# Second block: 28 feature-major projections as 14 seven-product pairs in a stage of their own, stored to DRAM, with the 32 gates dealt out 6, 10 and 16 over three mixers

## The chip, the cores and the metric

One core of one Trainium2 chip runs the whole program. The metric is device time in microseconds, the median of the runs of one kernel. Work is split over five engines: PE (matmul), with PEld for its weight loads, DVE, ACT, POOL and SP, which here issues the DMA transfers.

## The reference, cut to what matters

Two transformer blocks follow each other on x of 1024 tokens by 1024 features. The first (an mLSTM with window attention, then a convolutional FFN) is not touched. In the second, `xn = rmsnorm(x)` feeds one wide projection, and four mixers and four gates are computed from it:

```python
xn = rmsnorm_2(x, attn_norm_g)
proj = xn @ w_in                       # pool 512, dilated 3x768, stick 3x512, s5 512 columns
y_pool = pool_mixer(u_pool, pool_w, pool_scale)
y_dil  = dilated_attention(qkv_dil, rel_bias)     # 3 groups of 4 heads, dilation 1, 4, 16 (blocks of 128)
y_sb   = stick_breaking_attention(qkv_sb)         # 4 heads of 128
y_s5   = s5_mixer(u_s5, ...)
merged = 0
for bi, yb in enumerate((y_pool, y_dil, y_sb, y_s5)):
    gate = sigmoid(xn @ w_gate[bi])               # 1024 x 1024 each
    merged = merged + gate * (yb @ w_branch[bi])
x = x + merged @ w_out
hn = rmsnorm_2(x, ffn_norm_g); gu = hn @ w_up
x = x + (silu(gu[:, :F]) * gu[:, F:]) @ w_down    # F = 2816
return rmsnorm_2(x, final_norm_g)
```

## The kernel before, in words

**Layout and products.** x lies feature-major: eight tiles of 128 features by 1024 tokens. Every matmul is in float32 made of two rounded halves: a tile `t` is split into `hi` (rounded by ACT, L382) and `lo = t - hi` (DVE, L383), and a product is `hi*hi + hi*lo + lo*hi`, lines L358, L360 and L362 in `gemm`. A projection of 128 output features, from `load_w` (one 512 KB weight load, split in two halves of 512 columns) and `gemm`, is 8 x 3 x 2 = 48 matmuls of 512 columns. A gate, made by `gate` through `fill`, is 48 matmuls as well.

**The seven-product pair.** `pair` (L886) takes two such projections together: the two weight tiles are a 2 x 2 block matrix, the normed x another one (features 0 to 511 and 512 to 1023 by left and right half of the tokens), and the product of the two is made from seven half-size products of 12 matmuls each, 84 in all, where two projections by `gemm` are 96. For that POOL makes sums of weight blocks, and DVE adds the products up. The second FFN's `up` already runs 22 pairs this way.

**Order of the second block.** `block2_norm` (from L1566) normalises x, leaves its halves `xh`, `xl` and sends the residual `xd` to DRAM; it runs two half projections `early` ahead. Then come three mixers: `stick` (stick-breaking attention), `dilated`, and `s5`, in which the pool mixer runs along as a generator `means`. Then merge and FFN.

**Fills.** Where a mixer would leave PE waiting, the code calls `fill` (L300), which takes the next of the 32 gates off a list, computes it and spills it to DRAM. `stick` takes 1, `dilated` 15 and `s5` 16. The 28 feature-major projections (8 of `stick`, 12 + 4 of `dilated`, 4 of the pool mixer) stand between them and serve the same way. The order on each engine is fixed when the program is built: a scheduler, with priorities by place in the program, decides which matmuls of fills and projections stand between those of a mixer, and every engine then runs its list in order.

**The dilated mixer.** For each group g = 0, 1, 2 there is a setup: `oh,tab` matmuls (L1772) gather the relative bias, which is stored to a DRAM buffer (ED) and loaded back as `hk`; `hk` is transposed by PE (L1781); four `dqk` projections and, for g = 1 and 2, two `dvf` projections run, whose `dvf` tiles are transposed into `vd` by `turn`. The loop of eight steps n follows. One step is: scores on PE (L1850, four matmuls in the program, eight records in the trace); bias, maximum and sum on DVE (L1853, four, then L1856); four exps on ACT (L1858); four transposes on PE (L1863); a copy on ACT (L1866); the product with the values on PE (L1875); and copies out (L1878, L1880). In groups 0 and 1 most steps have 256 keys ("wide"), in group 2 all have 128 ("narrow"). A fill stands after every second step. After the loops `mst` is transposed (L1887), two more fills stand in group 2, and the weights of the groups (`E`, POOL, L1932) are spread by `E,selr` matmuls (L1943).

**s5.** Four quarters q: POOL builds `CL` (L2110) and `BL` (to L2134), PE transposes `BL` (L2140), DVE runs a recurrence to `H`, PE contracts it (L2211, L2212), then gelu and transposes. `CL` has one buffer, so the next quarter's POOL work starts when L2212 has read it. Each quarter has four gates or fewer and one step of the pool mixer, with its projection.

## Time and profile before

| what | value |
|---|---|
| median of 3 runs | 3456.14 us (3456.09 to 3456.77) |
| the profiled execution's own time | 3452.84 us |
| its span on the core | 3451.0 us |
| PE busy | 3312.0 us, 96% of the span |
| PEld, DVE, ACT, POOL busy | 76%, 61%, 38%, 19% |
| DMA | 348.60 MB, mean 101 GB/s |

The span is cut into stretches in the rows below: `block2_norm` ends about 1411 us, `stick` about 1659, `dilated` about 2112, `s5` (with its gated output) about 2490; the second FFN's norm is at 2741 to 2793, and its seven-product pairs from 2810 to 3170. A row of the busy times by stretch reads: from:to and length, then busy time of PE, PEld, DVE, ACT and POOL with the count of instructions, then the granted TensorE clock (1.00 is full), the DMA share and GB/s. A row of the timeline reads: start, duration, engine, line, operation, output<-input, shapes, and in brackets how long the engine was idle before it and what released it. In a row of one line's instructions, three durations in ns are the least, the median and the most.

### The profile page before, as it was taken

Reading aid. Unit: us, or ns where it says so; the run is one execution under the profiler, and the core shown is the slowest. Engines: PE = TensorE matmul, PEld = TensorE weight load, DVE = VectorE, ACT = ScalarE, POOL = GpSimd, SP = SyncE. Lnnn points to the kernel's source line nnn. Section 1 sums busy time; section 2 is a strip of 40 time slices with the busy share of each in tenths; the row PEclk is TensorE's granted clock in tenths of the full one; section 3 lists DMA queues with packets and bytes.
Section 4 is the critical chain, followed back from the end, with each engine's and each line's share of the span. In section 5 each row is a group of like instructions: output and inputs, shape, how many; then the busy total and the mean of one; then the engine's idle time right before and its main releaser. Section 6 shows DMA issues by size and latency. Waiting matters only on the chain. (4 is left out here: it accounts for less than half of the span.)

```text
span 3451.0 us, 42496 instructions
## 1 busy us (share of the span) xinstructions
PE 3312.0 (96%) x15699; PEld 2635.8 (76%) x15699; DVE 2092.2 (61%) x3955; ACT 1311.0 (38%) x2471; POOL 654.7 (19%) x510
## 2 busy tenths in 40 slices
PE   6999998989999999899999999999999989999998
PEld 4797776768888777777877778787878768888777
DVE  8746787686565797677332237466265764434886
ACT  5224655454444334356242332222222443333332
POOL 3200000152221441200000002221032142321530
PEclk9999999999999999999999999999999999999999
DMA  6545112422221432201121112222464322223232
GB/s 235 199 151 181 42 59 90 143 85 81 80 80 58 168 94 84 98 31 37 51 65 52 63 55 97 72 90 87 163 227 156 132 98 86 79 85 126 89 93 78
DMA packets 139953, 348.60 MB, mean 101 GB/s; under 512 B 16713, under 2 KB 41697, under 8 KB 139745
## 3 DMA queue, kind: packets, MB, share of 16 engines
q1 hardware_dynamic: 139744, 345.88, 29.7%
q8 instruction: 124, 2.03, 0.2%
q14 instruction: 85, 0.69, 0.1%
HBM read 270.67 MB, written 75.16 MB: 100 GB/s over the span
## 5 line engine op out<-in xcount | busy, mean ns | idle before, releaser
L382 ACT ACTIVATE wh<-w 128x512 fp32r<-128x512 f32 (+1 forms) x508 | 308.4, 610 | 1035.2 <-PE mm L360 734.5
L383 DVE TENSOR_TENSOR wl<-w,wh 128x512 fp32r<-128x512 f32 (+1 forms) x508 | 365.3, 723 | 512.6 <-ACT wh L382 491.5
L358 PE MATMUL mm<-bh,wh 128*128 128x512 f32 x1376 | 532.9, 401 | 26.7 <-ACT a L904 6.2
L362 PE MATMUL mm<-bh,wl 128*128 128x512 f32 x1376 | 523.6, 396 | 4.0 <-DVE wl L383 3.8
L360 PE MATMUL mm<-bl,wh 128*128 128x512 f32 x1376 | 526.3, 396 | 0.2 <-DVE bl L383 0.2
L358 PEld LDWEIGHTS mm<-bh,wh 128*128 128x128 f32 x1376 | 259.8, 189 | 110.2 <-DVE x L2364 11.7
L362 PEld LDWEIGHTS mm<-bh,wl 128*128 128x128 f32 x1376 | 259.7, 189 | 68.7 <-DVE wl L383 7.6
L362 PE MATMUL mm<-xh,wl 128*128 128x512 f32 x944 | 311.7, 401 | 0.0
L358 PE MATMUL mm<-xh,wh 128*128 128x512 f32 x944 | 308.9, 403 | 1.9 <-DVE sql L386 1.9
L360 PEld LDWEIGHTS mm<-bl,wh 128*128 128x128 f32 x1376 | 260.0, 189 | 57.8 <-DVE bl L383 0.6
L360 PE MATMUL mm<-xl,wh 128*128 128x512 f32 x944 | 304.1, 399 | 0.0
L896 POOL TENSOR_TENSOR ws<-w 128x512 f32<-128x512 f32 x44 | 67.0, 1523 | 850.3 <-DMA w<-in_w_up_dram 510.0
L362 PEld LDWEIGHTS mm<-xh,wl 128*128 128x128 f32 x944 | 176.8, 188 | 43.9 <-issue 5.8
L360 PEld LDWEIGHTS mm<-xl,wh 128*128 128x128 f32 x944 | 177.8, 189 | 40.8 <-issue 2.0
L358 PEld LDWEIGHTS mm<-xh,wh 128*128 128x128 f32 x944 | 174.3, 188 | 44.8 <-issue 5.1
L382 ACT ACTIVATE wh<-ws 128x512 fp32r<-128x512 f32 x176 | 110.7, 630 | 202.0 <-PE mm L360 171.9
L362 PE MATMUL ax<-bh,wl 128*128 128x512 f32 x416 | 165.3, 397 | 4.2 <-DVE wl L383 4.2
L360 PE MATMUL ax<-bl,wh 128*128 128x512 f32 x416 | 165.9, 399 | 2.2 <-DVE bl L383 2.1
L358 PE MATMUL ax<-bh,wh 128*128 128x512 f32 x416 | 165.8, 398 | 1.6 <-ACT bh L382 1.6
L383 DVE TENSOR_TENSOR wl<-ws,wh 128x512 fp32r<-128x512 f32 x176 | 137.6, 783 | 27.0 <-ACT wh L382 26.8
L1553 DVE SCALAR_TENSOR_TENSOR x<-mm,adaT,x 128x512 f32<-128x512 f32 (+1 forms) x104 | 85.4, 828 | 40.3 <-PE mm L362 40.0
L1932 POOL TENSOR_TENSOR E<-e,seld 32x1024 fp32r<-32x1024 f32 x3 | 8.2, 2733 | 476.8 <-issue 476.2
(639 smaller groups left out, 6849.9 us busy)
## 6 DMA issues: line engine op xcount, KB each, us to landing
w<-in_w_up_dram SPq DMA_DIRECT2D x88, 512.0 KB
wa<-in_w_ada_dram SPq DMA_DIRECT2D x64, 512.0 KB
w<-in_w_out_dram SPq DMA_DIRECT2D x32, 512.0 KB
w<-in_w_gate_dram SPq DMA_DIRECT2D x32, 512.0 KB
gd<-gf SPq DMA_DIRECT2D x32, 512.0 KB
g<-gd SPq DMA_DIRECT2D x32, 512.0 KB
y<-y SPq DMA_DIRECT2D x28, 512.0 KB
w<-in_w_down_dram SPq DMA_DIRECT2D x24, 512.0 KB
```

The source lines that it names most:

```text
L358: nc.tensor.matmul(ps, lhsT=wh, rhs=xh[k], start=s, stop=False, **kw)
L360: nc.tensor.matmul(ps, lhsT=wh, rhs=xl[k], start=False, stop=False, **kw)
L362: nc.tensor.matmul(ps, lhsT=wl, rhs=xh[k], start=False, stop=e, **kw)
L382: first = nc.scalar.activation(hi, src, AF.Copy)
L383: nc.vector.tensor_tensor(lo, src, hi.bitcast(F32), ALU.subtract)
L896: nc.gpsimd.tensor_tensor(t, x, y, op)
L1553: add = lambda m, x, ps: nc.vector.scalar_tensor_tensor(x, ps, self.adaT[:, 40 + m : 41 + m], x, ALU.mult, ALU.add)
L1932: eng.tensor_tensor(E.rearrange("p (n t) -> p n t", n=8), e.bitcast(F32).unsqueeze(1).to_broadcast([32, 8, P]), seld[:, 256:264].unsqueeze ...
```

## The change

`block2_norm` no longer runs `early` nor makes `xd`; it spills the raw x (`xr`), and prepares the operands of the seven products (`factors2`: B11, B21, T1, B22, T2, T3, T4, as in the second FFN). A new stage `project2` runs the 28 projections as 14 pairs, through `rows` (the loop that was in `up`). Each result is scaled, for the dilated mixer also reordered by dilation (ACT writes it token-residue major, and the store then has runs of 512 bytes for dilation 4, of 256 bytes for 8), and stored to DRAM. Between pairs `residual` loads `xr`, makes `xd` and stores it. The mixers load their inputs from DRAM where the projections stood. The constant GATES, by which gates could run in the new stage too, is empty. FILL says after which steps a fill stands in `dilated`: n = 1, 4 and 6 of each group, and one behind the groups, 10 in all; in `stick` 6 (one per head, and one more in heads 0 and 1); `s5` keeps 16.

```diff
...
+FILL = ((1, 4, 6), (1, 4, 6), (1, 4, 6), (0, 1))
+
+GATES = ()
...
     def block2_norm(self, xs, out):
...
-        def early(m):
-            hi, lo = self.load_w(A["w_sbqk"][m], D)
-            ps = self.pax()
-            self.gemm(hi, lo, [(ps, self.xh2[0], self.xl2[0])])
-            self.first.append((ps, hi, lo))
...
+                nc.sync.dma_start(self.xr[m][:, sl], xs[m][:, sl])
                 if h == 1:
-                    norm(m, 0)
-            if h == 1:
-                early(0)
-                early(4)
...
-        for k in range(KC):
-            self.dump(f"x2{k}", xs[k])
-            nc.vector.scalar_tensor_tensor(xs[k], xs[k], self.smc("final_norm", k), r1, ALU.mult, ALU.mult)
-            nc.sync.dma_start(self.xd[k], xs[k])
...
+    def project2(self, fp, B, steps):
...
+        jobs = [(sq(h), sq(4 + h)) for h in range(4)] + [(po(0), po(1)), (po(2), po(3))] + [(dq(2 * i), dq(2 * i + 1)) for i in range(6)] + [(dv(0), dv(1)), (dv(2), dv(3))]
+        jobs += [(ga(*GATES[i]), ga(*GATES[i + 1])) for i in range(0, len(GATES), 2)]
+
+        def run(j, *first):
+            def store(i, h, src):
+                _, d, scale, s, f = jobs[j][i]
+                if i == 0 and s == 1 and scale == 1.0 and f == AF.Copy:
+                    nc.sync.dma_start(d[:, h * HT : (h + 1) * HT], src)
+                    return
+                t = self.sm.tile([P, HT], F32, tag=("it", "dt")[h], name=self.nm("pj"), bufs=2)
+                nc.scalar.activation(t.rearrange("p (s l) -> p l s", s=s), src.rearrange("p (l s) -> p l s", s=s), f, scale=scale)
+                n = HT // s
+                nc.sync.dma_start(d.rearrange("p (s l) -> p s l", s=s)[:, :, h * n : (h + 1) * n], t.rearrange("p (s l) -> p s l", s=s))
...
+        def residual():
+            if left:
+                k = left.pop(0)
+                x = self.big("x")
+                nc.sync.dma_start(x, self.xr[k])
+                nc.vector.scalar_tensor_tensor(x, x, self.smc("final_norm", k), self.r1, ALU.mult, ALU.mult)
+                nc.sync.dma_start(self.xd[k], x)
...
+        self.rows(run, len(jobs), steps, residual)
...
@@ stick
                 if h < 3:
-                    qk, _ = heads(h + 1)
-                else:
-                    self.fill(None, turn=1, raw=True)
+                    qk, _ = heads(h + 1, fp)
+                self.fill(fp, turn=1, raw=True)
                 for _ in run[1]:
                     pass
+                if h in FILL[3]:
+                    self.fill(fp, turn=1, raw=True)
...
@@ dilated
                     for m in range(2):
-                        hi, lo = self.load_w(A["w_dvf"][2 * (g - 1) + m], D)
-                        ps = self.pmm()
-                        self.gemm(hi, lo, self.xtargets(ps, self.xh2, self.xl2))
                         t = self.big("dvf")
-                        nc.scalar.activation(t.rearrange("p (s l) -> p l s", s=dil), ps.rearrange("p (l s) -> p l s", s=dil), AF.Copy)
+                        nc.sync.dma_start(t, self.dvd[2 * (g - 1) + m])
...
                 for m in range(4):
-                    hi, lo = self.load_w(A["w_dqk"][4 * g + m], D)
...
+                    nc.sync.dma_start(t, self.dqd[4 * g + m])
...
-                if g == 0:
-                    self.fill(fp)
...
-                    if n % 2:
+                    if n in FILL[g]:
                         self.fill(fp)
...
                 if g == 2:
                     with tc.issue_after(last.ins):
-                        self.fill(fp)
                         self.fill(fp)
...
@@ pool mixer, in s5
         for g in range(4):
-            hi, lo = self.load_w(A["w_pool"][g], D)
-            ps = self.pmm()
-            self.gemm(hi, lo, self.xtargets(ps, self.xh2, self.xl2))
             u = self.big("u")
-            nc.scalar.activation(u, ps, AF.Copy)
+            nc.sync.dma_start(u, self.ud[g])
```

How this moves instructions is seen at two places. The first is PE in the loop of dilated group 2. Here is a part of one step of the kernel before: scores (L1850), transposes (L1863), and between them L358, L360 and L362, which are matmuls of a gate (`mm` from `xh`, `xl`).

```order
L1850 MATMUL ax_16619<-dk_16383,dq_16249 128x128
L1850 MATMUL ax_16618<-dk_16456,dq_16310 128x128
L1850 MATMUL ax_16619<-dk_16456,dq_16310 128x128
L362 MATMUL mm_16658<-xh_11165,wl_16651 128x512 x2
L358 MATMUL mm_16658<-xh_11166,wh_16650 128x512 x2
L360 MATMUL mm_16658<-xl_11174,wh_16650 128x512 x2
L362 MATMUL mm_16658<-xh_11166,wl_16651 128x512 x2
L1863 MATMUL ax_16633<-const,ds_16616 128x128
L358 MATMUL mm_16658<-xh_11167,wh_16654 128x512
L1863 MATMUL ax_16633<-const,ds_16616 128x128
```

And the same place in the changed kernel, where L1926 is the scores, L1939 the transposes and L1951 the product with the values; it is the start of group 2's loop, from the last `turn` (L1900) on.

```order
L1900 MATMUL ax_17343<-const,dvf_17317 128x128 x4
L1926 MATMUL ax_17355<-dk_17335,dq_17319 128x128
L1926 MATMUL ax_17356<-dk_17335,dq_17319 128x128
L1926 MATMUL ax_17355<-dk_17349,dq_17321 128x128
L1926 MATMUL ax_17356<-dk_17349,dq_17321 128x128
L1939 MATMUL ax_17370<-const,ds_17353 128x128 x4
L1951 MATMUL ax_17377<-dpt_17375,vd_17313 64x128 x4
L1926 MATMUL ax_17386<-dk_17335,dq_17319 128x128
```

From there to the end of group 2's eight steps no matmul of a gate stands on PE; before, 192 did. The three gates that the program text places in group 2's loop stand on PE ahead of it.

The second place is PE in the setup of group 2, around the transposes of `hk`, in the kernel before (L1781).

```order
L358 MATMUL mm_16139<-xh_11163,wh_16131 128x512 x2
L360 MATMUL mm_16139<-xl_11171,wh_16131 128x512 x2
L1781 MATMUL ax_16044<-hk_16042,const 128x256
L362 MATMUL mm_16139<-xh_11163,wl_16132 128x512
L1781 MATMUL ax_16050<-hk_16048,const 128x256
L362 MATMUL mm_16139<-xh_11163,wl_16132 128x512
L358 MATMUL mm_16139<-xh_11164,wh_16131 128x512 x2
```

In the changed kernel the transposes of `hk` are L1869.

```order
L362 MATMUL mm_17707<-xh_11170,wh_17703 128x512 x2
L364 MATMUL mm_17707<-xl_11178,wh_17703 128x512 x2
L366 MATMUL mm_17707<-xh_11170,wl_17704 128x512 x2
L1869 MATMUL ax_17291<-hk_17289,const 128x256
L1869 MATMUL ax_17297<-hk_17295,const 128x256
L1869 MATMUL ax_17303<-hk_17301,const 128x256
L1869 MATMUL ax_17309<-hk_17307,const 128x256
L1900 MATMUL ax_17323<-const,dvf_17315 128x128 x4
```

Between `oh,tab` and the first scores of group 2 stood 288 matmuls of gates and projections, 236 of them behind the first `hk` transpose; now 28 stand there, all ahead of it, and L1900 follows at once.

Counted in the same way over the whole dilated mixer, matmuls of gates and projections are, before and now: group 0 setup 193 and 37, loop 192 and 130; group 1 setup 288 and 50, loop 192 and 134; group 2 setup 288 and 28, loop 192 and 0; behind the groups up to `E,selr` 96 and 48. That is 1441 and 427.

## Rows read from the trace of the kernel before

**Rows 1.** Busy time by stretch: stick, dilated, s5, and the pairs of the FFN.

```profile
1411.00:1659.00 248.00, 245.49 (x1075) 183.26 (x1073) 168.30 (x356) 122.64 (x251) 4.79 (x8) 1.00 0.13 46
1659.00:2112.00 453.00, 450.87 (x2350) 346.94 (x2350) 136.32 (x378) 143.12 (x341) 8.20 (x3) 0.99 0.20 62
2112.00:2490.00 378.00, 374.42 (x1782) 310.41 (x1782) 211.28 (x633) 100.56 (x174) 65.71 (x81) 1.00 0.30 97
...
2810.00:3170.00 360.00, 359.65 (x1551) 291.12 (x1552) 150.44 (x229) 131.75 (x210) 97.34 (x71) 1.00 0.24 85
```

**Rows 2.** One line's instructions: SP's stores of each pair in the second FFN.

```profile
L1636 SPq EVENT_SEMAPHORE  x18: 17/7273/7276, 2838.4 to 3167.9; - x18
L1636 SPq DMA_DIRECT2D y<-a x18: 319/327/327, 2838.4 to 3169.4; - x18
```

**Rows 3.** One line's instructions: ACT's copies of two neighbouring projections.

```profile
L1807 ACT ACTIVATE dvf<-mm x2: 2020/2022/2023, 1817.0 to 1828.1; 128x1024 f32<-128x1024 f32 x2
```

**Rows 4.** Busy time by stretch: the norms ahead of stick and ahead of the FFN.

```profile
1375.00:1411.00 36.00, 26.62 (x115) 20.20 (x114) 33.67 (x43) 17.62 (x28) 21.43 (x13) 0.91 0.30 102
...
2741.00:2793.00 52.00, 43.28 (x176) 32.81 (x175) 47.36 (x68) 25.25 (x44) 19.61 (x12) 0.94 0.11 36
```

**Rows 5.** Timeline of PE: the `oh,tab` matmuls that open groups 0, 1 and 2.

```profile
1659.14 0.80 PE L1772 MATMUL ax<-oh,tab 32*4 32x384 f32 x2
...
1801.98 0.80 PE L1772 MATMUL ax<-oh,tab 32*4 32x384 f32 x2
...
1942.23 0.48 PE L1772 MATMUL ax<-oh,tab 32*4 32x384 f32 x1
```

**Rows 6.** One line's instructions: the scores of groups 0, 1 and 2.

```profile
L1850 PE MATMUL ax<-dk,dq x64: 272/376/480, 1730.4 to 1791.8; 64*128 64x256 f32 x56, 64*128 64x128 f32 x8
...
L1850 PE MATMUL ax<-dk,dq x64: 272/374/480, 1874.2 to 1931.8; 64*128 64x128 f32 x32, 64*128 64x256 f32 x32
...
L1850 PE MATMUL ax<-dk,dq x64: 272/272/374, 2013.6 to 2066.5; 64*128 64x128 f32 x64
```

**Rows 7.** Timeline of PE, DVE and ACT: one step of group 2.

```profile
2044.95 0.71 PE L1850 MATMUL ax<-dk,dq 64*128 64x128 f32 x8
...
2050.15 0.66 PE L1875 MATMUL ax<-dpt,vd 128*64 128x128 f32 x8
2050.74 0.71 PE L1850 MATMUL ax<-dk,dq 64*128 64x128 f32 x8
...
2045.88 0.28 DVE L1853 CUSTOM_DVE_ANT_0 ds<-ax,bias 128x128 f32<-128x128 f32 x1
...
2047.10 0.40 ACT L1858 ACTIVATE ds<-ds,nm 128x128 f32<-128x128 f32 x1 [0.95 <-DVE nm L1856]
...
2048.56 0.19 ACT L1858 ACTIVATION_READ_ACCUMULATOR ds<-ds,nm 128x1 f32 x1
...
2049.32 0.60 ACT L1866 ACTIVATE dpt<-ax 128x512 f32<-128x512 f32 x1 [0.57 <-PE ax L1863]
```

**Rows 8.** Timeline of PE: scores of two neighbouring wide steps of group 0.

```profile
1747.15 1.14 PE L1850 MATMUL ax<-dk,dq 64*128 64x256 f32 x8
...
1754.59 1.14 PE L1850 MATMUL ax<-dk,dq 64*128 64x256 f32 x8
```

**Rows 9.** One line's instructions: the `hk` transposes of group 2, ahead of its scores.

```profile
L1781 PE MATMUL ax<-hk,const x8: 378/379/454, 1955.1 to 1960.1; 128*128 128x256 f32 x8
```

**Rows 10.** Timeline of PE: the first of the `E,selr` matmuls that end dilated.

```profile
2098.12 0.50 PE L1943 MATMUL ax<-E,selr 32*128 32x512 f32 x1
```

**Rows 11.** Busy time by stretch: ten microseconds of the `E,selr` matmuls.

```profile
2101.00:2111.00 10.00, 9.74 (x22) 6.52 (x22) 10.00 (x14) 2.12 (x2) 0.00 (x0) 0.50 0.49 166
```

**Rows 12.** Timeline of POOL and PE: one quarter of s5.

```profile
2289.48 2.16 POOL L2110 TENSOR_TENSOR CL<-C,Lrs 128x1152 f32<-128x1152 f32 x1 [44.66 <-PE ax L2212]
...
2303.55 2.42 POOL L2134 TENSOR_TENSOR BL<-BL,BT 128x1024 f32<-128x1024 f32 x1
...
2312.80 0.27 PE L2140 MATMUL ax<-const,BL 128*128 128x128 f32 x1
...
2351.00 0.39 PE L2212 MATMUL ax<-CL,rt 128*128 128x128 f32 x2
```

More of the change, by code (lines that the diff above doesn't have):

```diff
@@ L966, in up, with rows @@
         run = lambda j, *first: self.pair(fp, W[j], W[NF + j], B, lambda a: hidden(j, a), gated, *first)
+        self.rows(run, NF, steps)
+        return out
+    def rows(self, run, n, steps, each=lambda: None):
         p, q = self.pmm(), self.pmm()
         g = [run(0, (p[:, 0:HT], q[:, HT:T])), run(1, (p[:, HT:T], None)), run(2, (q[:, 0:HT], None))]
-        for n in range(6):
-            if n > 1:
+        for i in range(6):
+            if i > 1:
                 next(steps)
-            for i in g:
-                next(i)
+            for r in g:
+                next(r)
         next(steps)
-        for i in g:
-            next(i)
+        for r in g:
+            next(r)
         cur = run(3)
@@ L979, in up @@
             next(cur)
-        for j in range(4, NF):
+        for j in range(4, n):
+            each()
             new = run(j)
@@ L988, in up @@
         next(cur)
-        return out
     def down(self, fp, W, xd, yd, add):
@@ new lines, in block2_norm, with factors2, split @@
+            row = self.rstd_twice(self.r1[:, sl], r2[:, sl], acc[:, 0:HT], acc[:, HT:T])
+        return B, self.factors2(xs, B, norm, row)
+    def factors2(self, xs, B, norm, row):
+        nc = self.nc
+        L, R = slice(0, HT), slice(HT, T)
+        sub = lambda eng, o, x, y: eng.tensor_tensor(o, x, y, ALU.subtract)
+        pairs = list(zip(xs[:4], xs[4:]))
+        def split(name, k, t):
+            if name not in B or len(B[name][0]) <= k:
+                pair = [self.half_tiles(2, n) for n in ("bh", "bl")]
+                for i in range(2):
+                    B.setdefault(name, ([], []))[i].extend(pair[i])
+            hi, lo = B[name]
+            self.split(t, hi[k], lo[k])
+        for k, (x, y) in enumerate(pairs):
+            norm(k, R, row)
+            nc.sync.dma_start(self.b12[k], x[:, R])
+            t = self.sm.tile([P, HT], F32, tag="it", name=self.nm("t1"), bufs=2)
+            sub(nc.vector, t, x[:, R], x[:, L])
+            split("T1", k, t)
+        yield
+        for k, (x, y) in enumerate(pairs):
+            norm(k + 4, R)
+            sub(nc.gpsimd, x[:, R], y[:, R], x[:, R])
+            split("B22", k, y[:, R])
+        yield
+        for k, (x, y) in enumerate(pairs):
+            nc.vector.tensor_tensor(x[:, L], x[:, R], x[:, L], ALU.add)
+            split("T2", k, x[:, L])
+        yield
+        for k, (x, y) in enumerate(pairs):
+            sub(nc.gpsimd, y[:, L], y[:, L], x[:, L])
+            split("T3", k, x[:, R])
+        yield
+        for k, (x, y) in enumerate(pairs):
+            split("T4", k, y[:, L])
+        yield
@@ L1833, in dilated @@
                         turn(m - 1)
-                nt = [self.big("num") for _ in range(2)]
-                if g == 0:
-                    self.fill(fp)
+                nt = [fp.tile([P, T], F32, name=self.nm("num")), self.big("num")]
                 for n in range(8):
```

89 lines of the change are left out of this document (50 added, 39 removed).

## The prediction

> **What bounds the kernel now.** I read the busy times by stretch first. In stick PE is busy 245.5 of 248.0 us, in dilated 450.9 of 453.0, in s5 374.4 of 378.0, and in the FFN's pairs 359.7 of 360.0 [rows 1]. So everywhere around the change the time is PE's work, and a matmul taken away seems to be worth its full price. But that table cannot say what PE would wait for if it had less to do. For this I read, second, the timeline of single steps in the mixers, where the matmuls of gates and projections stand inside chains of DVE and ACT work [rows 7, 8, 12], and third the order of PE before and now, which tells how many such matmuls are left in each place. The sum is then: work removed, less the waiting that the removed work had covered.
>
> **Work removed.** The price of a pair comes from the FFN's own pairs: its stores run from 2838.4 to 3169.4 us, 18 of them, so 331.0 / 17 = 19.47 us each [rows 2], which is 0.232 us for each of 84 matmuls. The price of a projection is the distance of two neighbours, 1828.1 − 1817.0 = 11.1 us for 48 matmuls [rows 3]. The new stage costs 14 × 19.47 = 272.6 us, the 28 projections that go cost 28 × 11.1 = 310.8 us: **−38.2 us**. The gates only move. Per matmul I use 0.2315 us.
>
> **The way into the pairs.** Before, PE idled 36.00 − 26.62 = 9.4 us in the stretch of the norm, with two half projections as cover. The analogue of the new way in is the FFN's norm with pairs behind it: 52.00 − 43.28 = 8.7 us idle [rows 4]. The new stage prepares its operands in the same steps. I put **0**, with bounds of −4 and +12: nothing can be won beyond half of the idle time there, and x is split and the raw x is stored in the same stretch, where DVE was busy 33.7 of 36.0 us.
>
> **Stores, loads, the residual.** The pairs of the FFN run with a DMA share of 0.24, ACT at 132 and DVE at 150 of 360 us [rows 1], so the four half stores of a pair, ACT's copies and the eight residual tiles (DVE, moved here from the norm) lie beside PE's work; without that cover they would cost a store issue of 0.33 us each [rows 2] and more. The loads in the mixers take the place of weight loads of the same size. I put 0; the bounds are 0 and the second rival below. The Trainium skill, "DMA: Bandwidth & Descriptors", Specifications, wants transfers of at least 512 bytes for line rate and says that below this the engines read, modify and write; that speaks against the stores for dilation 8 with their runs of 256 bytes, 3 of 14 pairs. By it these transfers would take longer, and the sum would move only if a later weight load then came late; no row of before shows such a store.
>
> **Stick.** Its share of gates and projections falls by some 140 matmuls with the two half projections ahead of it. PE was busy 99% [rows 1], the shortest blocks had 17 such matmuls before and have 16 to 38 now, so I take it that the rest still covers: no new waiting, ±6 us.
>
> **Dilated.** Here 1441 − 427 = 1014 matmuls go, 234.7 us of work. How much of it comes off the time, place by place:
> - *Group 2's loop.* All 192 go. A narrow step takes 2050.74 − 2044.95 = 5.79 us [rows 7], with 16 matmuls of a gate in it, 3.70 us; PE's own part is 2.09 us. But the step is a chain: scores at 2044.95, DVE from 2045.88, ACT's exps from 2047.10 to about 2048.75, the last transpose, ACT's copy from 2049.32, the values at 2050.15 [rows 7]. Only some 0.3 us in it is PE busy with other matmuls while the next operand is there. In the new order the next scores stand behind this step's values, so steps cannot overlap. I put 5.45 us for a step without gates, between 5.2 and 5.79: PE then waits 5.45 − 2.09 = 3.36 us in each, **+27** over eight steps (25 to 30).
> - *Group 2's setup.* It takes 2013.6 − 1942.2 = 71.4 us [rows 5, 6], of which 288 matmuls are 66.7 us. 28 are left, so PE's work is 4.7 + 6.5 = 11.2 us. But the bias goes to DRAM and back: the last `hk` transpose starts at 1960.1 [rows 9], 17.9 us after `oh,tab`, and the `turn` transposes and DVE's copies come behind. I put 21 us, so **+10** of waiting; between +2 (the chain is shorter once no weights are split beside it) and +14.
> - *Groups 0 and 1.* 427 − 28 − 48 = 351 matmuls are left there, and a wide step of 1754.59 − 1747.15 = 7.44 us [rows 8] has more work of PE's own. The gates cover the loops nearly: **+3**, between 0 and 10.
> - *Behind the groups.* 48 of 96 matmuls go, 11.1 us, ahead of the `E,selr` matmuls at 2098.12 [rows 10], which wait for a chain over DMA and POOL. Half of it comes off: **+5.5**, between 0 and 11.
>
> Waiting added in dilated: **+45.5**, so 189 of 234.7 us come off.
>
> **s5.** Four projections go, 44.4 us. In one quarter POOL runs from 2289.48 to 2303.55 + 2.42 = 2305.97, and PE comes to its result at 2312.80 [rows 12]: 6.8 us of slack. From there to L2212 at 2351.0 I take DVE's recurrence to set the pace, and the next quarter's POOL work waits for that L2212. So a quarter can shrink by 6.8 us, not by 11.1. Three times 4.3 is 12.9, and I add 1.6 in the last quarter's tail: **+14.5**, between 6 and 20. The gates keep their places.
>
> **Sum.** −38.2 + 0 + 0 + 45.5 + 14.5 = +21.8; by the ends of the waits alone it runs from about −5 to +47. Against the profiled execution's own 3452.84 us that is 3474.6; this execution lies 3.3 us under the median of the runs, 3456.14, so the forecast is **3478 us**. A measurement of this kernel tells about 0.2%, 6.9 us, from no change.
>
> **The clock.** In ten microseconds of the `E,selr` matmuls the granted clock was 0.50, the lower of its two levels, 1.2 instead of 2.4 GHz, though PE counts as busy 9.7 of 10 us; in the stretches with full cover it was 0.99 to 1.00 [rows 1, 11]. In group 2's loop PE will work 2.1 of 5.4 us. If it ran there at half clock, the scores, the last transpose and the values of each step would lengthen by some 1.1 us, 9 us in eight steps: 3486. The Trainium skill, "TensorE: Matmul & The Clock Gate", in the section "HAM oscillation", says that a loop which waits between short bursts of matmuls falls back to the lower clock again and again. By that rule this rival would hold rather than the full clock of my sum; the rows do not decide it.
>
> **The rivals.**
> 1. *Faster: the chains shorten when the weight splits leave ACT and DVE.* Every gate or projection brings ACT and DVE splits, which stand between the mixer's own steps. If without them a narrow step takes 3.6 us (waiting 12 instead of 27), the setup loses 2 and s5 6, and the end nothing, then waiting is 23 and the sum −15: about 3441. It decides from 38 us of waiting downwards. For it: no row shows these chains alone. Against it: in the step shown, ACT's and DVE's own pieces follow each other almost without a gap [rows 7]. Chance 0.14.
> 2. *The new stage is held back by its stores.* SP waits up to 7.27 us for a pair's result before it issues the store [rows 2], and now four stores per pair, some in short runs, stand in the queue ahead of the next weights. If that delays each pair by 1 to 2 us, it costs 14 to 28: 3491 to 3505. For it: one queue for all, and a pair stores two tiles where the FFN's stores one, with the residual's traffic beside it. Against it: PE lost 0.35 us in 360 with the same queue [rows 1]. Chance 0.12.
> 3. *Half clock* in the loop of group 2, as above: 3486. Chance 0.06.
> 4. *No difference:* s5 and the setup keep their cover, as the gates that the scheduler moved ahead happen to suffice, and waiting is 30 to 45: 3449 to 3463. Chance 0.12.
> 5. *The change does not do what it says:* FILL names steps 1, 4 and 6 of group 2, but no gate stands in that loop. This is in the order already and thus in my sum; it is the main reason for the loss.
>
> My own case has 0.56.
>
> **How the numbers follow.** Slower by over 0.2% is my case with rivals 2 and 3: 0.74; within 0.2% is rival 4: 0.12; faster is rival 1: 0.14. The range of 8 in 10 leaves out most of rival 1 (below 3451) and the far end of rival 2 (above 3500): 3451 to 3500. The own range of my case is 3463 to 3493.
>
> **What the profile after would show.** The stores of the new stage should be 19.5 us per pair apart. PE should be busy about 2.1 us in a narrow step of 5.3 to 5.6 us; the time from the first scores of group 2 to the last should be near 7 × 5.45 = 38 us, instead of 52.9. `oh,tab` to the first scores of group 2 should take about 21 us, PE waiting for `hk` or for DVE's `vd`. In s5 PE should wait for POOL's `BL` in each quarter, and a quarter should last near 54 us. PE's idle time between the norm and the merge should have grown by 50 to 70 us. I am wrong if the narrow step falls below 4 us, if PE stays busy over 95% in s5, or if the pairs of the new stage are over 20.5 us apart.

## The result

The changed kernel takes 3505.07 us (3499.85 to 3514.63 in 4 runs) where the kernel before takes 3456.11: slower, ratio 1.0150 (95% interval 1.0123 to 1.0177). The forecast was 3478 in a range of 3451 to 3500: the right sign, but 27 us too little, and the time lies above the range. The profiled execution took 3502.51 us.

Its rows in the order of the program. First the timeline of PE in the profile after, at the places that cut the span: first matmul of stick (L1727), first `oh,tab` of group 0 and of group 2, first `E,selr`, first product of s5's gated output.

```profile
1690.75 0.40 PE L1727 MATMUL ax<-wth,xh 128*128 128x512 f32 x1
...
1916.85 0.48 PE L1860 MATMUL ax<-oh,tab 32*4 32x384 f32 x1
...
2086.63 0.48 PE L1860 MATMUL ax<-oh,tab 32*4 32x384 f32 x1
...
2171.02 0.50 PE L2018 MATMUL ax<-E,selr 32*128 32x512 f32 x1
...
2479.70 0.40 PE L362 MATMUL mm<-y5h,wh 128*128 128x512 f32 x1
```

The kernel before has the same instructions at 1659.14 and 1942.23 [rows 5], at 2098.12 [rows 10], and the first and last of the five here, in the same view of its trace:

```profile
1411.13 0.50 PE L1630 MATMUL ax<-wth,xh 128*128 128x512 f32 x1
...
2434.37 0.39 PE L358 MATMUL mm<-y5h,wh 128*128 128x512 f32 x1
```

Subtracting gives where the 49.1 us of span went (3500.1 against 3451.0):

| stretch | before | after | change | forecast |
|---|---|---|---|---|
| start to stick (norm, and now the pairs) | 1411.1 | 1690.8 | +279.6 | +261.5 |
| stick | 248.0 | 226.1 | −21.9 | −21.3 |
| dilated, to `E,selr` | 439.0 | 254.2 | −184.8 | −189.2 |
| `E,selr` and s5 | 336.3 | 308.7 | −27.6 | −29.9 |
| the rest | 1016.7 | 1020.4 | +3.7 | 0 |

(+261.5 is 272.6 for the pairs less 11.1 for the two half projections that stood in the norm; −21.3 is the prediction's some 140 matmuls, less the 48 of those halves, at 0.2315 us.) So two thirds of the miss, 18 us, lie in one line: on the way into the pairs or in them. Busy times by stretch of the profile after, with the columns of [rows 1]:

```profile
1411.00:1690.00 279.00, 269.85 (x1143) 215.29 (x1143) 135.86 (x177) 129.52 (x203) 78.43 (x56) 0.99 0.40 132
1690.00:1917.00 227.00, 224.94 (x986) 166.84 (x986) 153.56 (x336) 127.04 (x252) 4.38 (x8) 1.00 0.23 79
1917.00:2171.00 254.00, 221.70 (x1299) 162.88 (x1297) 79.55 (x310) 89.33 (x277) 2.67 (x1) 0.88 0.24 79
...
2260.00:2480.00 220.00, 209.68 (x1058) 166.43 (x1058) 149.89 (x455) 59.92 (x91) 45.28 (x59) 0.99 0.31 102
...
2097.00:2160.00 63.00, 38.17 (x186) 24.98 (x187) 15.98 (x87) 21.20 (x80) 0.00 (x0) 0.55 0.08 24
```

Stick keeps PE busy as forecast. Dilated now has 32 us without PE work and a granted clock of 0.88; in group 2's setup and loop, the last row, it is 0.55. s5 idles 10 us.

The pairs themselves are as forecast. The timeline of ACT shows the last store copy of two neighbouring pairs:

```profile
1648.79 1.15 ACT L1676 ACTIVATE pj<-v 128x512 f32<-128x512 f32 x1 [0.24 <-DVE v L908]
...
1668.31 1.14 ACT L1676 ACTIVATE pj<-v 128x512 f32<-128x512 f32 x1 [0.24 <-DVE v L908]
```

That is 19.52 us per pair (forecast 19.47), and the last ten distances between pairs are all 19.52 to 19.57 us, those with short store runs among them. So the 18 us lie ahead of the steady pairs. The waits of PE there, 1376 to 1455 us (engine, line, released by: us in all, times, longest), are these:

```profile
PE mm L362 <- DVE x L1563: 4.3, 3, 1.8
PE ax L434 <- DVE y L465: 4.1, 1, 4.1
PE mm L366 <- DVE wl L387: 3.7, 2, 2.0
PE ax L366 <- DVE wl L387: 3.0, 1, 3.0
PE mm L362 <- ACT a L909: 2.8, 1, 2.8
```

Most wait for DVE: for block 1's own additions, for the root of the norm, for weight splits. The timeline of DVE right behind the norm, a split (L387), a scaling (L1593) and three splits in a row:

```profile
1423.76 0.68 DVE L387 TENSOR_TENSOR wl<-ws,wh 128x512 fp32r<-128x512 f32 x1
...
1426.73 1.78 DVE L1593 SCALAR_TENSOR_TENSOR x<-x,gg,r 128x512 f32<-128x512 f32 x1
1428.43 1.78 DVE L387 TENSOR_TENSOR xl<-x,xh 128x512 fp32r<-128x512 f32 x1
1430.14 1.76 DVE L387 TENSOR_TENSOR xl<-x,xh 128x512 fp32r<-128x512 f32 x1
1431.82 0.68 DVE L387 TENSOR_TENSOR xl<-x,xh 128x512 fp32r<-128x512 f32 x1
```

A split takes 0.68 us in the first and the last row, and 1.78 and 1.76 in between, 1.35 on the mean of the second to the fourth split (the expectations below use such means). POOL works beside those two:

```profile
1427.92 1.75 POOL L1615 TENSOR_TENSOR x<-x,x 128x512 f32<-128x512 f32 x1
1429.63 1.72 POOL L1615 TENSOR_TENSOR x<-x,x 128x512 f32<-128x512 f32 x1
```

These two POOL instructions end at 1429.67 and 1431.35, and each of the two slow splits ends some 0.55 us behind one of these ends, at 1430.21 and 1431.90.

In group 2 a narrow step got longer than the 5.45 us that I had put. The timeline of PE:

```profile
2118.92 1.23 PE L1926 MATMUL ax<-dk,dq 64*128 64x128 f32 x8
2122.07 1.63 PE L1939 MATMUL ax<-const,ds 128*128 128x128 f32 x4 [1.92 <-ACT ds L1934]
2124.38 1.12 PE L1951 MATMUL ax<-dpt,vd 128*64 128x128 f32 x8 [0.69 <-ACT dpt L1942]
...
2125.43 1.23 PE L1926 MATMUL ax<-dk,dq 64*128 64x128 f32 x8
...
2060.51 0.72 PE L1926 MATMUL ax<-dk,dq 64*128 64x128 f32 x8
2065.97 1.13 PE L1926 MATMUL ax<-dk,dq 64*128 64x256 f32 x8
```

6.51 us in group 2, with 1.23 us for scores that took 0.71 [rows 7]; but 5.46 us for the narrow step of group 1 in the last two rows, at 0.72. In s5 PE now waits for POOL, as forecast. The timeline of PE, first transpose of `BL` in the second quarter:

```profile
2322.10 0.33 PE L2215 MATMUL ax<-const,BL 128*128 128x128 f32 x1 [1.76 <-POOL BL L2209]
```

### The profile page after: what moved, and what is told of

Read it like the earlier page. It is cut to its first block, busy times and chain, and to the rows that moved or that the text cites. A ratio compares the mean times of both kernels' runs of the same rounds, so it can differ in the third digit from the quotient of the medians.

```text
span 3500.1 us, 42902 instructions
## 1 busy us (share of the span) xinstructions
PE 3308.0 (95%) x15531; PEld 2626.0 (75%) x15531; DVE 2170.9 (62%) x4063; ACT 1393.2 (40%) x2610; POOL 727.0 (21%) x566
## 2 busy tenths in 40 slices
DMA packets 172019, 388.46 MB, mean 111 GB/s; under 512 B 30856, under 2 KB 61984, under 8 KB 171808
## 5 line engine op out<-in xcount | busy, mean ns | idle before, releaser
L362 PE MATMUL mm<-bh,wh 128*128 128x512 f32 x1544 | 599.4, 400 | 31.1 <-ACT a L909 9.0
L366 PE MATMUL mm<-bh,wl 128*128 128x512 f32 x1544 | 589.3, 396 | 4.3 <-DVE wl L387 4.3
L364 PE MATMUL mm<-bl,wh 128*128 128x512 f32 x1544 | 593.0, 396 | 0.2 <-DVE bl L387 0.2
L387 DVE TENSOR_TENSOR wl<-w,wh 128x512 fp32r<-128x512 f32 (+1 forms) x494 | 359.9, 733 | 357.3 <-ACT wh L386 338.2
L362 PEld LDWEIGHTS mm<-bh,wh 128*128 128x128 f32 x1544 | 291.7, 189 | 123.1 <-ACT a L909 11.9
L387 DVE TENSOR_TENSOR wl<-ws,wh 128x512 fp32r<-128x512 f32 x232 | 179.4, 776 | 70.1 <-ACT wh L386 70.0
L362 PE MATMUL mm<-xh,wh 128*128 128x512 f32 x616 | 214.1, 406 | 4.2 <-ACT gf L2363 2.0
L364 PE MATMUL mm<-xl,wh 128*128 128x512 f32 x616 | 213.9, 407 | 0.0
L366 PE MATMUL mm<-xh,wl 128*128 128x512 f32 x616 | 210.7, 403 | 0.0
L362 PE MATMUL ax<-bh,wh 128*128 128x512 f32 x416 | 165.7, 398 | 1.6 <-ACT bh L386 1.6
L362 PEld LDWEIGHTS mm<-xh,wh 128*128 128x128 f32 x616 | 116.2, 191 | 32.7 <-issue 2.6
L364 PEld LDWEIGHTS mm<-xl,wh 128*128 128x128 f32 x616 | 116.2, 191 | 29.3 <-issue 6.1
L366 PEld LDWEIGHTS mm<-xh,wl 128*128 128x128 f32 x616 | 116.1, 191 | 27.4 <-issue 3.2
L901 POOL TENSOR_TENSOR ws<-ws,w 128x512 f32<-128x512 f32 x58 | 78.0, 1345 | 203.7 <-DMA w<-in_w_up_dram 152.3
```

The source lines that it names most:

```text
L362: nc.tensor.matmul(ps, lhsT=wh, rhs=xh[k], start=s, stop=False, **kw)
L364: nc.tensor.matmul(ps, lhsT=wh, rhs=xl[k], start=False, stop=False, **kw)
L366: nc.tensor.matmul(ps, lhsT=wl, rhs=xh[k], start=False, stop=e, **kw)
L387: nc.vector.tensor_tensor(lo, src, hi.bitcast(F32), ALU.subtract)
L901: nc.gpsimd.tensor_tensor(t, x, y, op)
```

## The experiments

Times are medians, ratios against the kernel before with their 95% intervals. The kernel before had medians of 3456.3 to 3458.0 in the later comparisons. Places are read from each run's trace. The norm's first sum (first `ones,acc` matmul) lies between 1355.7 and 1363.9 us from profile to profile, though nothing ahead of it was changed; so the lead-in is counted from there to stick's first product: 52.9 us before, 333.5 in the changed kernel (331.9 and 332.8 in two kernels below with the same lead-in). Less 14 x 19.52 us of pairs, and before less the half projections' 11.1, it is 60.2 against 41.8: the loss in question is **18.4 us**. The norm's first sum in the timeline of PE, before and, below it, after; stick's first products are shown above:

```profile
1358.26 0.39 PE L421 MATMUL ax<-ones,acc 128*128 128x2 f32 x2 [0.78 <-POOL acc L413]
...
1357.30 0.49 PE L425 MATMUL ax<-ones,acc 128*128 128x2 f32 x3 [0.78 <-POOL acc L417]
```

**Cover in group 2 back (g2_in_place).** "Cover" is work of PE that stands where it would otherwise wait. Nothing is left out of the computation; the edit is cut to its main lines.

```diff
-jobs: ... dq 0..11 in six pairs, dv 0..3 in two pairs
+jobs: ... dq 0..7 in four pairs, dv(0), dv(1) in one
...
 dilated, g == 2:
-    nc.sync.dma_start(t, self.dqd[4 * g + m])
+    hi, lo = self.load_w(A["w_dqk"][4 * g + m], D); ps = self.pmm(); self.gemm(...)
```

> Edit: the six projections of dilated group 2 stand in the mixer again, by gemm, as in the kernel before; 11 pairs are left. Theory A (the loss in dilated is PE waiting in group 2 once its cover is gone, part of it at half clock): work rises by 8 us (288 matmuls for three pairs); the loop of group 2 goes back from 51.6 us to about 57 to 62 with 144 matmuls of gates in it, the setup to about 70 with 288 more in setup and loop together, and PE's waiting there falls from 43 us to under 5; the time falls by 30 to 38 us, to about 3470. Theory B (the loss is the lead-in of the pairs alone, and group 2 would wait anyway, for its DRAM loads and copies): waiting in group 2 stays over 25 us and the time stays above 3490. The lead-in is the same in both.

3474.14 us, 1.0050 (1.0035 to 1.0065): 31 us faster than the changed kernel, although PE has 8 us more to do. From `oh,tab` to the end of the loop group 2 takes 95.4 us with 300 matmuls of projections and gates, where it took 71.4 with 28; 24 us for 63 us of work. Theory A holds, at the lower end of the gain that it gave; the loop (54.1 us) and the setup (41.3) came out shorter than its 57 to 62 and about 70.

**Only the gates moved (gates_only).**

```diff
 kernel before:
+FILL = ((1, 4, 6), (1, 4, 6), (1, 4, 6), (0, 1)), used in stick and dilated as in the change; no pairs
```

> Edit: the kernel before with only the gates dealt out anew, 6 in stick, 10 in dilated, 16 in s5; all 28 projections stay in the mixers, no pairs. It computes the same. Theory A (projections taken out are what uncovers the mixers; the gates' places alone do little): the projections still cover, group 2's setup keeps 271 matmuls and its loop 144; 3456, between 3450 and 3463. Theory C (the new distribution of the gates is itself what costs): group 2's loop, with 144 instead of 192 matmuls, and the part behind the groups wait, and the time is 3470 or more.

3470.55 us, 1.0041 (1.0026 to 1.0056): A missed, and C came as forecast, so dealing out the gates anew costs some 13 us by itself. Stick grew by 55.6 us, the full price of the 240 matmuls that came to it, while dilated shrank by only 50.5; the `E,selr` matmuls with the start of s5's first quarter took 97.7 us instead of 91.4. That last piece is 97.7 in the changed kernel as well, so 6 us of its loss hang on the moved gates, not on the pairs.

**Gates held in place (pinned).**

```diff
-                    if n in FILL[g]:
+                    if n in FILL[g] and g < 2:
                         self.fill(fp)
+                    elif n in FILL[g]:
+                        with tc.issue_after(pvi.ins):   # last product with the values
+                            self.fill(fp)
```

> Edit: the changed kernel, with the three gates of group 2 held back until the products with the values of steps 1, 4 and 6, so that they do stand in its loop. 144 matmuls are then in that loop, 18 instead of 134 in the loop of group 1, none in the setup of group 2. Theory A (there is not enough cover, wherever it stands): group 2's steps come back to full clock and PE is busy in them, its loop stays at 50 to 56 us; group 1's loop can fall only to its own chain, about 48 us from 53; the setup of group 2 stays at 18 to 20 us. Sum: 0 to 8 us faster, 3497 to 3505. Theory D (the cover suffices, the scheduler only puts it in the wrong place): 20 us or more faster, below 3485.

3556.64 us, 1.0296 (1.0279 to 1.0313). No theory had this. The three gates stand in the loop as unbroken lumps between two steps: a step with one takes 19 to 20 us, about 6 plus more than a gate's whole 11.1, so they cover nothing. And group 1's loop, now nearly without gates, took 63.1 instead of 53.2 us, with 9.45 us for a wide step instead of 7.43. Group 1's loop by busy time, in pinned and, below it, in the changed kernel:

```profile
2039.60:2102.70 63.10, 41.74 (x228) 26.77 (x227) 17.21 (x84) 23.93 (x81) 0.00 (x0) 0.66 0.14 50
```

```profile
2033.10:2086.30 53.20, 53.20 (x343) 38.03 (x342) 19.75 (x88) 27.92 (x87) 0.00 (x0) 1.00 0.29 100
```

The granted clock is 0.66 where it was 1.00. In these loops cover helped only between the instructions of a step; where it was missing the loop paid more than its chain at full clock.

**Unread work in group 2 (warm).** The added products are read by nobody; the output is the same.

```diff
+                    if g == 2:
+                        pw = self.pax()
+                        with tc.issue_after(sc.ins):
+                            for i in range(11):
+                                nc.tensor.matmul(pw, lhsT=self.xh[0][:, 0:P], rhs=self.xh2[i % 2][1], start=True, stop=True)
```

> Edit: the changed kernel with 11 matmuls of 512 columns, whose result nobody reads, behind the scores of each step of group 2 (88 in all, 20 us of work at full clock). The rest of the order is the same. Theory E (the narrow step there lasts 6.51 us and not 5.46, as in group 1, because TensorE runs at half clock): from the second or third step on the granted clock is 1.00 and a step lasts 5.4 to 5.6 us, the loop falls from 51.6 to 45 to 47 us, though 20 us of work were added. Theory F (it is something else, such as loads or the copies with a stride of eight): a step stays at 6.5 us or gets longer. The time changes by -6 us in E, by 0 to +8 in F.

3501.11 us, 1.0132 (1.0117 to 1.0147), 4 us faster by the medians, with ranges that overlap, so the reading rests on the trace: the loop itself fell from 51.6 to 43.3 us. Its timeline of PE, one step:

```profile
2120.68 0.71 PE L1926 MATMUL ax<-dk,dq 64*128 64x128 f32 x8
2121.32 2.84 PE L1931 MATMUL ax<-xh,xh 128*128 128x512 f32 x11
2124.00 0.80 PE L1944 MATMUL ax<-const,ds 128*128 128x128 f32 x4
2125.49 0.66 PE L1956 MATMUL ax<-dpt,vd 128*64 128x128 f32 x8 [0.69 <-ACT dpt L1947]
2126.07 0.71 PE L1926 MATMUL ax<-dk,dq 64*128 64x128 f32 x8
...
2090.00:2155.00 65.00, 53.68 (x324) 39.49 (x322) 18.14 (x93) 22.74 (x82) 0.00 (x0) 0.95 0.11 35
```

The last row is the stretch by busy time: clock 0.95 instead of 0.55. A step takes 5.39 us with 2.8 us of extra work in it, 6.51 without. Theory E is shown: with the clock back the whole excess over my 5.45 us is gone. The rule on this from the Trainium skill, "TensorE: Matmul & The Clock Gate", "HAM oscillation", that I had weighed against the sum, holds here.

**The lead-in: DVE's load (lo_pool) and the DMA queue (xr_act).**

```diff
 lo_pool, in the norm's loop:
-                    self.split(xs[m][:, L], self.xh2[0][m], self.xl2[0][m])
+                    nc.scalar.activation(self.xh2[0][m], xs[m][:, L], AF.Copy)
+                    nc.gpsimd.tensor_tensor(self.xl2[0][m], xs[m][:, L], self.xh2[0][m].bitcast(F32), ALU.subtract)
 xr_act:
-                nc.sync.dma_start(self.xr[m][:, sl], xs[m][:, sl])
+                nc.scalar.dma_start(self.xr[m][:, sl], xs[m][:, sl])
```

> Edit: the changed kernel, with the low halves of the left tokens' x in the norm made on POOL, as in the kernel before, and no longer on DVE (eight of 0.68 us). The lead-in, the way from block 1's last products into the new stage, costs 17.6 us more PE pauses in the changed kernel than in the one before. Theory G (DVE has too much to do in the lead-in): the first product of stick comes 4 to 8 us earlier, 3497 to 3501. Theory H (DVE is slowed by POOL working beside it, 1.3 instead of 0.7 us for such an operation; or the lead-in waits for weights): nothing gained or 1 to 5 us lost.

> Edit: the changed kernel, with the spills of the raw x issued from ACT's queue instead of SP's. Theory Q (in the lead-in the weights of the first pairs come late, because their loads stand on SP behind spills of x that wait for DVE; ACT waited 4.7 us and POOL 7.4 us for such a weight): the third weight load is issued at about 1370 to 1375 us instead of 1387.8, POOL's sums start before 1385 instead of 1394.6, and the first product of stick comes 5 to 12 us earlier; 3493 to 3500. Theories G and H (DVE and POOL set the lead-in): within 2 us of the changed kernel.

lo_pool: 3509.76 us, 1.0150 (1.0135 to 1.0166); its lead-in is 338.4, 5 us longer with less on DVE: G falls. xr_act: 3511.53 us, 1.0158 (1.0143 to 1.0173); lead-in 331.5, no change against the 331.9 to 333.5 of its kind. SP's list is free of the spills now, and POOL's first sum of weights starts 34.5 us behind the norm's first sum instead of 37.3; nothing came of it. But the third weight load moved less than Q asked: it is issued 27.6 us behind the first sum instead of 30.5, as it now waits 18.2 us for DVE's weight split, which still reads the buffer that it fills. So the spills were not what held it, and Q falls as stated; whether earlier weights would help stays untested.

**The lead-in: cover (no_early, after_early).**

```diff
 no_early, kernel before:
-                early(0)
-                early(4)
 after_early, changed kernel, ahead of the norm's root:
+                for b, m in self.todo[:2]:
+                    hi, lo = self.load_w(self.A["w_gate"][b, m], D)
+                    ps = self.pax()
+                    self.gemm(hi, lo, [(ps, self.xh2[0], self.xl2[0])])   # left half; stick's fill adds the right half
...
```

> Edit: the kernel before, without its two half projections ahead in the norm (48 matmuls, 11.1 us); the two projections run whole in stick. It computes the same. Theory C (these were the cover of the norm, and the changed kernel has lost it): the same work runs later, the norm's PE pauses grow from 13.0 us by 8 to 11, and the time goes to 3464 to 3467. Theories G and Q: the pauses grow by less than 4 us, as other work of block 1 lies beside the norm; within 5 us of 3457.

> Edit: the changed kernel, with the left halves of two gates (24 matmuls each) computed in the norm, where the kernel before has its two half projections, and only their right halves later in stick; the two gates' weights are loaded and split twice. Theory C (the lead-in lost its cover): PE's pauses there fall from 30.6 us to 18 to 22, the first product of stick comes at about the same time although 11.1 us of work were moved ahead of it, stick is 11 us shorter, and the time falls by 8 to 12 us, to 3493 to 3497. Theory G (DVE sets the lead-in): four more weight splits on DVE lengthen it, pauses stay at 27 or more, and less than 3 us are gained.

no_early: 3469.42 us, 1.0039 (1.0024 to 1.0054): the way that C said, and beyond its 3464 to 3467. Its lead-in is 57.3 where 41.8 is left without the two halves' own work: 15.5 us lost by nothing but taking them out. Its timeline of PE, from the norm's first sum to stick's first product:

```profile
1357.79 0.38 PE L421 MATMUL ax<-ones,acc 128*128 128x2 f32 x2 [0.78 <-POOL acc L413]
...
1399.58 0.79 PE L358 MATMUL mm<-xh,wh 128*128 128x512 f32 x1 [15.17 <-ACT wh L382]
...
1415.10 0.77 PE L1627 MATMUL ax<-wth,xh 128*128 128x512 f32 x1
```

after_early: 3504.24 us, 1.0139 (1.0123 to 1.0154): within 1 us of the changed kernel. 11.1 us of work lengthened its lead-in by 5.7 us, so cover did something there, and stick gave back 9.9. That is 4 us gained in the two profiles, and 3.3 of it are lost again ahead of the norm's first sum (1360.60 against 1357.30), where nothing was changed; the medians cannot tell 4 us from nothing. So the halves are worth 15.5 us of lead-in in the kernel before, and as new half gates 5.4 (11.1 less 5.7) in the changed one, where something else sets most of the lead-in.

**The lead-in: POOL beside DVE (sub_dve, no_pool_lead).**

```diff
 sub_dve, in factors2, twice:
-            sub(nc.gpsimd, ...)
+            sub(nc.vector, ...)
 no_pool_lead, also, in pair, for the first three pairs of the stage:
-            nc.gpsimd.tensor_tensor(t, x, y, op)
+            nc.vector.tensor_tensor(t, x, y, op)
```

> Edit: the changed kernel, with the eight differences of x in the preparation of the operands on DVE instead of POOL. In the changed kernel POOL works on them for 13.6 us, in two stretches in which DVE's operations take about 1.35 instead of 0.68 us. Theory H (POOL beside it slows DVE, and DVE's list is what PE waits for after the norm): DVE gets 5.4 us of work and loses about 7 of slowing, and the chain from POOL to ACT gets shorter; PE's pauses after the norm, 1424 to 1455 us, fall from about 10 to 5 or less, the first product of stick comes 2 to 5 us earlier, counted from the norm's first sum. Theory G (DVE simply has too much to do): no gain, or up to 5 us lost.

> Edit: sub_dve, and the twelve weight sums of the first three pairs on DVE too, so that POOL does nothing between the norm's sums and the fourth pair. DVE gets 13.6 us more work, none of it slowed. Theory H: the small operations of the norm's square root on DVE, five of which took 1.2 instead of 0.2 us, take 0.2 us again, the pause of 4.3 us there shrinks to about 1, and the lead-in is no longer than in sub_dve or shorter. Theory G: the lead-in gets 6 to 13 us longer than in the changed kernel.

sub_dve: 3503.0 us, 1.0130 (1.0115 to 1.0145), lead-in 327.8, 5.7 shorter. no_pool_lead: 3498.07 us, 1.0119 (1.0102 to 1.0136), lead-in 320.6, **12.9 shorter with 13.6 us more work on DVE**. G forecast 6 to 13 longer. The whole kernel is 7 us faster than the changed one by the medians, and the intervals of the two ratios overlap; the same two edits are tried again below, with nine pairs. The ends of this lead-in, in the timeline of PE:

```profile
1362.78 0.38 PE L427 MATMUL ax<-ones,acc 128*128 128x2 f32 x2 [0.78 <-POOL acc L419]
...
1683.39 0.39 PE L1731 MATMUL ax<-wth,xh 128*128 128x512 f32 x1
```

The timeline of DVE in no_pool_lead, to set beside that of the changed kernel:

```profile
1424.04 0.69 DVE L389 TENSOR_TENSOR xl<-t,xh 128x512 fp32r<-128x512 f32 x1
...
1427.11 0.68 DVE L1617 TENSOR_TENSOR x<-x,x 128x512 f32<-128x512 f32 x1
1427.71 0.68 DVE L389 TENSOR_TENSOR xl<-x,xh 128x512 fp32r<-128x512 f32 x1
1428.32 1.41 DVE L1595 SCALAR_TENSOR_TENSOR x<-x,gg,r 128x512 f32<-128x512 f32 x2
...
1404.42 0.16 DVE L464 TENSOR_SCALAR v<-t 128x4 f32<-128x4 f32 x1
```

Splits and scalings take 0.68 and 0.7 us again, and the root's small operation of the last row 0.16 us, in the changed kernel 1.24. The timeline of DVE there, and of POOL beside it:

```profile
1402.16 1.24 DVE L462 TENSOR_SCALAR v<-t 128x4 f32<-128x4 f32 x1
...
1401.66 1.72 POOL L901 TENSOR_TENSOR ws<-w 128x512 f32<-128x512 f32 x1
```

The DVE operation ends at 1403.40, right behind the end of POOL's at 1403.38. Four of the root's operations are slow in this way (the expectation says five). The pause before the root's transposes fell only from 4.1 to 2.4 us, not to about 1.

The stretch from 1376 to 1480 us by busy time, the changed kernel and, below it, no_pool_lead:

```profile
1376.00:1480.00 104.00, 84.36 (x333) 64.23 (x332) 86.87 (x111) 46.82 (x83) 52.64 (x35) 0.90 0.38 129
```

```profile
1376.00:1480.00 104.00, 92.62 (x382) 71.22 (x381) 87.96 (x138) 53.85 (x96) 24.23 (x17) 0.93 0.38 136
```

DVE counts as busy for 87 to 88 us in both, and gets 138 instructions done instead of 111. H is shown: POOL's work there cost 12.9 us of lead-in. How much of this is DVE held up, and how much the shorter way through a sum (0.68 us on DVE, 1.26 to 1.72 on POOL), is not separated. The Trainium skill, "SBUF — State Buffer", "Who interferes with whom", says that a DVE instruction with two inputs in SBUF contends with a POOL instruction that reads SBUF, over ports that are an exclusive lock; the two slow splits above, which end 0.55 us behind POOL's, agree. The other 5.5 us of the 18.4 are about what the half gates brought in after_early (5.4); best_nine, below, tries both together.

**Fewer pairs.** The next kernels keep pairs only where PE needs no cover: nine_pairs also has the pool mixer's projections in place; nine_end puts a second gate behind the dilated groups again, out of stick; nine_end_early adds after_early's half gates, nine_end_early_sub also sub_dve, best_nine also no_pool_lead; best_nine_noend is best_nine without nine_end's move.

```diff
 nine_pairs, on g2_in_place:
-jobs: ... [(po(0), po(1)), (po(2), po(3))]
...
 pool mixer:
-            nc.sync.dma_start(u, self.ud[g])
+            hi, lo = self.load_w(A["w_pool"][g], D); ps = self.pmm(); self.gemm(...)
 nine_end:
-FILL: stick (0, 1)
+FILL: stick (0,), and two fills behind the groups
```

> Edit: group 2's six projections in the mixer, as in g2_in_place (3474.1), and the pool mixer's four as well; 9 pairs are left. Theory A (cover): two pairs of 19.5 us go, four projections of 11.1 us come back, but s5 gets only 30 us longer for 44 of work, since its quarters waited 4 us each and its end: 9 us faster than g2_in_place, 3462 to 3468, still slower than the kernel before because of the lead-in. Rival (s5's quarters are set by POOL and DVE alone): s5 gets 44 us longer and it is 5 us slower, 3479.

> Edit: nine_pairs (3465.8), with one gate moved from stick to the place behind the dilated groups, where two stand then, as in the kernel before. Theory A (cover): behind the groups and in the E,selr matmuls one gate fewer saved only 3.4 of 11.1 us, so the move gains 6 to 8 us there if stick has cover enough without it: 3458 to 3460. Rival (stick misses that gate, or the chain behind the groups is no shorter with it): within 2 us of nine_pairs.

> Edit: nine_end and after_early together: nine pairs, two gates behind the groups, two half gates in the norm. If C and A hold and add up: 3466 - 7 - 10 = 3449, between 3445 and 3453, faster than the kernel before (3456). If the half gates only take cover from stick, or DVE sets the lead-in, 3457 to 3461.

> Edit: nine_end_early (3457.6) with the differences of x on DVE as in sub_dve. If sub_dve gains and the half gates are cover beside it: 3452 to 3455, just faster than the kernel before. If sub_dve gains nothing: 3456 to 3460.

> Edit: nine pairs, two half gates in the norm, two gates behind the dilated groups (as nine_end_early), and POOL kept out of the lead-in as in no_pool_lead. Theory H adds: nine_end_early_sub was 3449.9; the weight sums on DVE gave 5 to 7 us beyond sub_dve in the changed kernel: 3442 to 3446, faster than the kernel before by 0.3 to 0.45%. Rival (with the half gates' splits on DVE too, DVE is now full, and its extra work shows): 3449 to 3455.

> Edit: best_nine with one gate again in stick instead of behind the dilated groups. The move gained nothing in nine_end (3465.1 against 3465.8), so within 3 us of best_nine; if stick misses that gate with the half gates gone from it too, best_nine_noend is 3 to 6 us faster.

| kernel | us | ratio to before |
|---|---|---|
| nine_pairs | 3465.79 | 1.0030 (1.0020 to 1.0039) |
| nine_end | 3465.06 | 1.0022 (1.0012 to 1.0033) |
| nine_end_early | 3457.58 | 1.0001 (0.9992 to 1.0011) |
| nine_end_early_sub | 3449.85 | 0.9975 (0.9964 to 0.9985) |
| best_nine | 3443.69 | 0.9960 (0.9945 to 0.9975) |
| best_nine_noend | 3447.26 | 0.9970 (0.9960 to 0.9979) |

nine_pairs came out as A said. nine_end is a miss: stick got 13.4 us shorter, but from the last step to s5's first quarter 9.1 came back, and 3.6 in group 2's setup. Why that place takes nearly the full price of a gate is open. In best_nine the move comes out 3.6 us better, which the intervals do not tell from nothing. nine_end_early is 7.5 us faster than nine_end by the medians, but not through its half gates as far as the traces show: of the 8.4 us between the two profiled executions 7.7 lie ahead of the norm's first sum (1355.67 against 1363.39), where nothing was changed, and 0.7 behind it. The last two steps came the way that H forecast, nine_end_early_sub 2 us below its 3452 to 3455. From nine_end_early to best_nine, which are the two edits of no_pool_lead, the medians fall by 13.9 us, with intervals well apart, and the lead-in by 14.6 (242.9 to 228.3); that confirms H on the whole time. best_nine's lead-in, less 9 x 19.52 us of pairs and the half gates' 11.1, is 41.5 us, where the kernel before has 41.8 and nine_pairs 59.3: POOL's work given to DVE and the half gates together bring back the whole loss of the lead-in (best_nine_noend, with the same lead-in, has 43.8, so a figure of this kind is good to some 2 us). best_nine beats the kernel before by 0.40% (0.25 to 0.55%). Its lead-in stretch by busy time shows PE at 97 of 104 us at a clock of 0.97:

```profile
1376.00:1480.00 104.00, 96.93 (x414) 75.60 (x414) 86.91 (x140) 55.73 (x100) 20.47 (x15) 0.97 0.38 137
```

## Why the prediction was wrong

- **Work removed:** right. A pair costs 19.52 us, put at 19.47; so −38.2 stands. The second rival, stores that hold the stage back, did not come: packets under 512 bytes went from 16713 to 30856 in the two profiles, and the spacing of the pairs shows nothing of it. So the rule of the Trainium skill, "DMA: Bandwidth & Descriptors", Specifications, that I had set against the change did not reach the time.
- **The way into the pairs:** here the prediction failed. I put 0, with a bound of +12, from the idle time of the FFN's norm [rows 4]; it cost 18.4. The rows that I compared end before the first pairs are through, and two things had no price in my sum. One is POOL's work: I read "DVE was busy 33.7 of 36.0 us" as a load, but beside POOL DVE is held up, and the stage puts its sums of weights and differences of x, on POOL, right there; on DVE they made the lead-in 12.9 us shorter. The other is the cover of the two half projections: I took them off as 11.1 us of plain work, and without them the kernel before loses 15.5 us of lead-in (no_early). In the changed kernel the second weighs less, 5.4 us (after_early), and the two add up to 18.3; with both made good the loss is gone (41.5 against 41.8, best_nine).
- **Stick:** right, −21.9 against −21.3.
- **Dilated:** the mechanism was right, one term was mis-sized. Against 234.7 us of work removed 184.8 came off: 49.9 of waiting, put at 45.5. The loop of group 2 cost +34 instead of +27, since the step took 6.51 us: 5.45 was right as the chain at full clock (5.46 in group 1, 5.39 in warm), and the third rival's price of 1.1 us a step for half clock was right as well, but I gave it a chance of 0.06 as an alternative when it belonged in the sum. The setup of group 2 cost 8.6 (put at 10), groups 0 and 1 about 6 (put at 3), the part behind 1.6 (put at 5.5).
- **s5:** nearly right, −27.6 with the `E,selr` matmuls, put at −29.9. The wait for `BL` and quarters of 54.4 to 56.2 us (54 forecast) are in the trace. But a sign that I had set for being wrong, PE busy over 95% in s5, is there too (209.68 of 220.00 us): it was badly set, as my own 14.5 us of waiting leave PE 95% busy in these 309 us.
- **The rest:** +3.7 us after s5, not forecast and not explained; in the runs above that part varies between 1016 and 1025 us.
- The first rival (chains that shorten) did not come: the narrow step kept its 5.4 us.

The sum of the misses, 18.1 − 0.6 + 4.4 + 2.3 + 3.7 = 27.9, makes up the difference between 3474.6, forecast for the profiled execution, and its 3502.51, to within 1 us: the forecasts by stretch add up to 21.1, and my sum was 21.8.

## What to carry to other kernels

A matmul that stands between the instructions of a waiting chain costs little (in group 2, 24 us for 63 us of such work); saving it, or moving it to a stage of its own, saves as little, and can drop the clock of what is left: count the cover of each loop before and after, step by step. Save work where PE is the limit on its own (nine of these fourteen pairs), and leave plain products where chains wait. At a transition where DVE is the engine waited for, look at what POOL does beside it: with the same work on DVE alone the lead-in was 13 us shorter.

## What the runs showed of the hardware

- DVE beside POOL: a split of 128x512 took 0.68 us alone and 1.78 beside POOL's subtractions, ending 0.55 us behind the end of one; a 128x4 operation took 0.16 and 1.24. Giving DVE POOL's 20 sums and differences there was faster.
- TensorE's clock: in group 2's loop, where PE waits for ACT twice in every step, the granted clock was near its lower level (0.55 over the stretch), and 88 unread matmuls, 20 us of work, shortened the loop by 8.3 us. In group 1's loop the clock fell as well once its gates were gone (0.66 over the loop, and 9.45 instead of 7.43 us for a wide step, in pinned).
